# Scaling an expert's gathered token rows on ScalarE beside their transposes, in place of GpSimd behind the gather

## Chip, core and metric

The kernel is one program on one core of a Trainium2 chip. TensorE (PE, with its weight loads as PEld), VectorE (DVE), ScalarE (ACT), GpSimd (POOL) and the DMA queues of SyncE (SP) and GpSimd run side by side, each with its own list of instructions in a fixed order. The metric is the device time of one execution in microseconds (us).

## What is computed

A hybrid mixer block, then two layers of which the second ends in a mixture of experts; only that last part is touched by the change:

```
logits = t @ router_w;  top_logits, top_idx = top_k(logits, 2);  top_w = softmax(top_logits)
gates  = sum over k of top_w[:, k] * one_hot(top_idx[:, k])          # 512 tokens x 8 experts
for e in range(8):
    y = y + gates[:, e:e+1] * ((silu(t @ wg[e]) * (t @ wu[e])) @ wd[e])
```

`t` (512 x 1024) is an RMS norm of the residual rows times a column weight plus a column shift, and `wg`, `wu` are 1024 x 1408, `wd` is 1408 x 1024, all float32.

## The kernel before, in words

**Tokens are gathered by expert.** The normalised rows are written to a DRAM buffer `hnd` without their norm factor. For each expert a list of its token numbers (`ii`) and one norm factor for each token (`sc`) are made on chip. `fetch` (L1552) issues an indirect DMA on GpSimd's queue for each tile of tokens, which gathers the tokens' rows of 4 KB from `hnd` into `row`, 128 or 64 tokens by 1024. Then the rows are multiplied by `sc`: on GpSimd at L1563, or, for the first expert only (`now`), on ScalarE and VectorE. `inputs` (L1635) transposes `row` on TensorE, 16 blocks of 128 columns or fewer, and ScalarE and VectorE split the result into `eh` (high part) and `el` (low part).

**Two sizes of expert, taken in turns.** The experts are sorted by how many tokens they have. The first four have 192 places, as tiles of 128 and 64 (wide below); the last four have one tile of 128 (narrow). They are taken in the order `(0, 4, 1, 5, 2, 6, 3, 7)`, so a wide one and a narrow one take turns. During an expert the tokens of the one after it are prepared: `prepare(nxt)` and `fetch` stand in the program behind block `b == 0` (L1724), and `inputs` behind the first half of the last product (`m == 0`, L1742). A narrow expert so fetches two tiles, and a wide one fetches one.

**One expert.** Gate and up products run in three column blocks of 512, 512 and 384 (`b`). Each block takes eight weight chunks (`raw`, 128x1024, and 128x768 for the last block), and the down product takes twelve. `wload` (L235) does the same for each chunk: SP starts the load, ScalarE rounds it to `hi` (L205), VectorE makes `lo = raw - hi` (L216), TensorE multiplies by `hi` and by `lo`. There are 8 buffers for `raw` and 4 each for `hi` and `lo`. After a block ScalarE takes the silu of the gate (named `eh` too in the records, 128x512 from `g`), VectorE multiplies it by up (`eh<-g,eh`), and TensorE transposes the product (L1716 `m<-cst,eh`) for the down product (`th`, `tl`). The result is scaled and added into DRAM by an indirect DMA of GpSimd (`yd<-row`, L1755).

**What sets the order.** A scheduler puts each engine's instructions in a list when the program is built, with the chunk's load, `hi` and `lo` at high priority. On the chip an engine takes its list as it stands.

Of the kernel before, what the change touches and what calls it, by code (L numbers as in the profile page):

```python
# [13 lines left out]
AF = mybir.ActivationFunctionType  # L14
OP = mybir.AluOpType
# [4 lines left out]
D = 1024  # L20
# [154 lines left out]
def tile_kernel(ctx, tc, I, out, dbg=None, upto=99):  # L175
    nc = tc.nc
# [13 lines left out]
    def G(n=512):  # L190
        return pg.tile([128, n], F, tag="g", name="g")
# [5 lines left out]
    def act(o, i, f, bias=None, scale=None, accum=None):  # L197
        kw = {}
        if bias is not None:
            kw["bias"] = bias  # L200
        if scale is not None:
            kw["scale"] = scale
        if accum is not None:
            kw["accum_out"] = accum
        return nc.scalar.activation(out=o, in_=i, func=f, **kw).ins  # L205

    def stt(o, a, s, b, op0, op1):
        return nc.vector.scalar_tensor_tensor(out=o, in0=a, scalar=s, in1=b, op0=op0, op1=op1).ins  # L208

    def ts(o, a, s1, s2=None, op0=OP.mult, op1=None):  # L210
        if op1 is None:
            return nc.vector.tensor_scalar(out=o, in0=a, scalar1=s1, scalar2=None, op0=op0).ins
        return nc.vector.tensor_scalar(out=o, in0=a, scalar1=s1, scalar2=s2, op0=op0, op1=op1).ins
# [21 lines left out]
    def wload(src, n, after=()):  # L235

        fast["i"] += 1
        i = fast["i"]
        with ExitStack() as order:
            order.enter_context(tc.high_priority())  # L240
            for a in after:
                order.enter_context(tc.issue_after(a))
            p = fast["raw"] if fast["raw"] is not None and i % 2 else rawp
            raw = p.tile([128, 1024], F, tag="raw", name="raw")
            d = nc.sync.dma_start(out=raw[:, 0:n], in_=src)
            if i <= KD:
                tc.keep_in_program_order(d)
            hi = wsp.tile([128, 1024], R, tag="hi", name="hi")
            lo = wsp.tile([128, 1024], R, tag="lo", name="lo")
            act(hi[:, 0:n], raw[:, 0:n], AF.Copy)  # L250
            tt(lo[:, 0:n], raw[:, 0:n], hi[:, 0:n].bitcast(F), OP.subtract)
        return hi, lo
# [945 lines left out]
    with ExitStack() as st:  # L1198
# [321 lines left out]
        def dispatch(pays, n0, n, OH, a=0, b=8):  # L1520
            ps = M(8)[0:n]
            mm(ps[:, a:b], idb[:, 0:n], cw[:, n0 // 128, a:b], True, False)
            for t in range(NT):
                mm(ps[:, a:b], OH[:, t, n0:n0 + n], pays[:, t, a:b], False, t == NT - 1)
            return ps
# [3 lines left out]
        def slots(n, ps, real):  # L1529

            ii = lp.tile([n, 1], I32, tag=f"ii{n}", name="ii", bufs=3)
            with nc.allow_low_precision("small integers"):
                last[0] = nc.vector.reduce_sum(out=ii, in_=ps[:, 0:2], axis=AX.X).ins
            fi = None
            if real:
                fi = lp.tile([n, 1], F, tag=f"fi{n}", name="fi", bufs=2)
                nc.vector.reduce_sum(out=fi, in_=ps[:, 0:2], axis=AX.X)
            sc = lp.tile([n, 1], F, tag=f"sc{n}", name="sc", bufs=3)
            nc.vector.reduce_sum(out=sc, in_=ps[:, 2:5], axis=AX.X)
            return ii, fi, sc  # L1540
# [11 lines left out]
        def fetch(tiles, now=False):  # L1552

            for t_ in tiles:
                nc.gpsimd.indirect_dma_start(out=t_[4], out_offset=None, in_=hnd,
                                             in_offset=bass.IndirectOffsetOnAxis(ap=t_[2][:, 0:1], axis=0))
            for t_ in tiles:
                r, sc = t_[4], t_[5]
                if now:
                    act(r[:, 0:512], r[:, 0:512], AF.Copy, scale=sc[:, 0:1])  # L1560
                    ts(r[:, 512:1024], r[:, 512:1024], sc[:, 0:1])
                else:
                    nc.gpsimd.tensor_tensor(out=r, in0=r, in1=sc[:, 0:1].to_broadcast([t_[0], D]), op=OP.mult)  # L1563

        def places(P, W, off=0.0):
            OH = lp.tile([128, NT, 192], BF, tag="OH", name="OH", bufs=1)
# [4 lines left out]
        def prepare(r):  # L1571
            W = 192 if r < 4 else 128
            OH = places(P1r[:, r, :], W)
            return [tile_of(pay[:, r], n0, min(128, W - n0), OH, r == 7) for n0 in range(0, W, 128)]
# [5 lines left out]
        for n0, n in ((0, 128), (128, 64)):  # L1580
            ii, fi, sc = slots(n, dispatch(pay[:, 0], n0, n, OH0, 0, 5), False)
# [37 lines left out]
    with ExitStack() as st:  # L1619
# [3 lines left out]
        def hw(tag, shape=(128, T), dt=F):  # L1623
            return hp.tile(list(shape), dt, tag=tag, name=f"e{tag}")
# [10 lines left out]
        def inputs(tiles):  # L1635

            xs, pins = [], []
            for t_ in tiles:
                if t_[0] == 128:
                    e = wk.tile([128, 8, 128], R, tag="eh", name="eh", bufs=2)  # L1640
                    xs.append(([e[:, 0:4, :], e[:, 4:8, :]], two(("l2", "l3", "l4", "l5"))))
                else:
                    xs.append((two(("l6", "l7", "h6", "h7")), None))
            for m in range(2):
                for t_, (eh, el) in zip(tiles, xs):
                    n, xg = t_[0], t_[4]
                    ps = M(4 * n)
                    for k in range(4):
                        z = 512 * m + 128 * k
                        nc.tensor.transpose(ps[:, n * k:n * k + n], xg[:, z:z + 128], ident[0:n, 0:n])  # L1650
                    pv = ps.rearrange("p (k t) -> p k t", t=n)
                    hi, lo = (eh[m], el[m]) if n == 128 else (eh[m][:, :, 0:64], eh[m][:, :, 64:128])
                    b = [B[:, 4 * m + k:4 * m + k + 1] for k in range(4)]
                    for k in range(4):
                        pa = act(hi[:, k, :], pv[:, k, :], AF.Identity, bias=b[k])
                    for k in range(4):
                        pd = stt(lo[:, k, :], pv[:, k, :], b[k], hi[:, k, :].bitcast(F), OP.add, OP.subtract)
                pins.append((pa, pd))
            return xs, pins

        def emm(ps, a, b, hi, lo, first, last):
            mm(ps, a, hi, first, False)
            mm(ps, a, lo, False, last and b is None)
            if b is not None:
                mm(ps, b, hi, False, last)

        def whole(ps, n):

            lo = hw("h3")[0:64, 0:n]
            act(lo, ps[64:128, 0:n], AF.Copy)  # L1670
            turn["s"] = 1 - turn.get("s", 0)
            o = hw(("h4", "h5")[turn["s"]])[0:64, 0:n]
            tt(o, ps[0:64, 0:n], lo, OP.add)
            return o

        def expert(e, tiles, out_, nxt=None, beside=None):
# [10 lines left out]
            after = None  # L1687
            for b, w in enumerate((512, 512, 384)):
# [17 lines left out]
                for i, n in enumerate(ns):  # L1706
# [7 lines left out]
                    m = w // 128  # L1714
# [9 lines left out]
                if b == 0:  # L1724
                    if nxt is not None:
                        after = [prepare(nxt)]
                        fetch(after[0])
            yts = [row(n) for n in ns] if out_ is None else None
            for m in range(2):
                yp = [G() for n in ns]  # L1730
                for k0 in range(0, 11, 2):
                    kn = min(2, 11 - k0)
                    src = I["e_d"][bass.ds(e, 1), m, :, 512 * k0:512 * (k0 + kn)]
                    hi, lo = wload(src.rearrange("a p n -> (a p) n"), 512 * kn)
                    for r in range(kn):
                        k = k0 + r
                        z = slice(512 * r, 512 * r + 512)
                        for i in range(len(ns)):
                            th, tl = hs[i]
                            emm(yp[i], th[:, k, :], tl[:, k, :] if tl is not None else None, hi[:, z], lo[:, z],  # L1740
                                k == 0, k == 10)
                if m == 0 and after is not None:  # L1742
                    after.append(inputs(after[0]))
                for i, n in enumerate(ns):
                    p = yp[i] if n == 128 else whole(yp[i], 512)
                    iw = tiles[i][1][:, 0:1]
                    if out_ is None:
                        stt(yts[i][:, 512 * m:512 * m + 512], p, iw, g2[m][0:n], OP.mult, OP.mult)
                    else:
                        y = hw("h1")  # L1750
                        stt(y, p, iw, g2[m], OP.mult, OP.mult)
                        out_(m, y, tiles[i])
            if out_ is None:
                for i, n in enumerate(ns):
                    nc.gpsimd.indirect_dma_start(  # L1755
                        out=yd, out_offset=bass.IndirectOffsetOnAxis(ap=tiles[i][2][:, 0:1], axis=0),
# [134 lines left out]
```

## Time and profile before

| What | Value |
|---|---|
| Median of three runs | 1772.07 us (1770.12 to 1777.74) |
| The profiled execution | 1773.76 us, of which the span from first to last instruction is 1771.9 us |
| TensorE busy | 1717.7 us, 97% of the span |
| VectorE, ScalarE, GpSimd busy | 1234.7, 852.8, 78.6 us |
| Mean granted TensorE clock | 0.989 |

A busy time is the union of an engine's instructions; the end of a matmul is modelled, so a row's start says more than its end. The arrow in a row's brackets, as `[1.36 <-DVE lo L216]`, gives the engine's idle time ahead of that instruction and what ended it. `hi`, `lo`, `row` are names of tiles without their buffer numbers, and L205, L208, L212, L216, L219 are the lines of helpers, so that instructions are told apart by their tiles.

### The profile page before, as it was taken

What the parts mean: (1) busy time and instruction counts of PE and PEld (TensorE: products, weight loads), DVE (VectorE), ACT (ScalarE), POOL (GpSimd) and SP (SyncE); (2) the same over time, 40 slices, a digit from 0 to 9 for tenths busy, and PEclk for the clock granted to TensorE, in tenths of its full rate; (3) what the DMA queues carried; (4) which work ended last, traced back from release to release, by engine and by line L of the source; (5) the groups of instructions that cost most, each with busy time, mean ns of one, the idle gap of its engine ahead of it and who ended that gap; (6) DMA issues with size and microseconds to landing.
All of it is one profiled execution on the core that took longest, in us unless ns stands there. A gap on an engine that the chain in (4) does not pass through costs nothing. (4 is left out here: it accounts for less than half of the span.)

```text
span 1771.9 us, 24089 instructions
## 1 busy us (share of the span) xinstructions
PE 1717.7 (97%) x8580; PEld 1411.9 (80%) x8580; DVE 1234.7 (70%) x2065; ACT 852.8 (48%) x1326; POOL 78.6 (4%) x90
## 2 busy tenths in 40 slices
PE   8999998998999999999999999999999999999996
PEld 7867787786788888888888888787887887887884
DVE  6887789857567666443346766646788789788787
ACT  5435336745443222232333222535667567567575
POOL 1000001000000000000010000000011011011000
PEclk9999999999999999999999999999999999999998
DMA  8434641344426777333242111106789789789785
GB/s 270 137 112 136 226 126 59 118 153 158 132 88 221 250 240 244 115 98 91 97 142 73 48 60 60 48 24 244 258 279 339 228 281 334 228 283 338 228 282 226
DMA packets 95701, 313.47 MB, mean 177 GB/s; under 512 B 10772, under 2 KB 11284, under 8 KB 95576
## 3 DMA queue, kind: packets, MB, share of 16 engines
q1 hardware_dynamic: 89864, 295.88, 50.1%
q0 software_dynamic: 3408, 11.80, 3.1%
q10 hardware_dynamic: 2304, 4.20, 0.6%
q8 instruction: 69, 1.13, 0.3%
q14 instruction: 56, 0.46, 0.1%
HBM read 299.25 MB, written 12.58 MB: 176 GB/s over the span
## 5 line engine op out<-in xcount | busy, mean ns | idle before, releaser
L205 ACT ACTIVATE hi<-raw 128x1024 fp32r<-128x1024 f32 (+3 forms) x481 | 477.5, 996 | 592.8 <-PE g L219 474.4
L216 DVE TENSOR_TENSOR lo<-raw,hi 128x1024 fp32r<-128x1024 f32 (+3 forms) x481 | 551.5, 1158 | 288.0 <-ACT hi L205 278.0
L219 PE MATMUL g<-xh,hi 128*128 128x512 f32 (+1 forms) x912 | 354.8, 391 | 10.5 <-ACT hi L205 5.4
L219 PE MATMUL g<-xl,hi 128*128 128x512 f32 (+1 forms) x912 | 356.1, 391 | 1.0 <-DVE xl L208 0.8
L219 PE MATMUL g<-xh,lo 128*128 128x512 f32 (+1 forms) x912 | 356.4, 391 | 0.0
L219 PEld LDWEIGHTS g<-xh,hi 128*128 128x128 f32 x912 | 172.6, 190 | 45.2 <-ACT xh L205 6.0
L219 PEld LDWEIGHTS g<-xl,hi 128*128 128x128 f32 x912 | 173.0, 190 | 36.5 <-DVE xl L208 2.4
L219 PEld LDWEIGHTS g<-xh,lo 128*128 128x128 f32 x912 | 172.9, 190 | 33.4 <-issue 1.1
L219 PE MATMUL g<-lo,eh 128*128 128x512 f32 (+1 forms) x480 | 180.9, 377 | 4.7 <-DVE lo L216 4.7
L219 PE MATMUL g<-hi,eh 128*128 128x512 f32 (+1 forms) x480 | 180.1, 376 | 0.0
L219 PE MATMUL g<-hi,el 128*128 128x512 f32 (+1 forms) x480 | 167.1, 379 | 0.0
L378 DVE SCALAR_TENSOR_TENSOR ar<-ar,one,crow 128x1024 f32<-128x1024 f32 x96 | 122.1, 1283 | 29.0 <-DMA ar<-in_ada_dram 26.4
L219 PEld LDWEIGHTS g<-lo,eh 128*128 128x128 f32 x480 | 90.4, 188 | 19.6 <-DVE lo L216 5.6
L219 PE MATMUL g<-hi,th 128*128 128x512 f32 x264 | 105.0, 398 | 0.2
L219 PE MATMUL g<-lo,th 128*128 128x512 f32 x264 | 103.7, 393 | 0.0
L219 PEld LDWEIGHTS g<-hi,eh 128*128 128x128 f32 x480 | 90.5, 189 | 14.1
L219 PEld LDWEIGHTS g<-hi,el 128*128 128x128 f32 x480 | 90.0, 189 | 13.5
L219 PE MATMUL g<-fh,hi 128*128 128x512 f32 (+1 forms) x198 | 73.1, 369 | 0.0
L219 PE MATMUL g<-fl,hi 128*128 128x512 f32 (+1 forms) x198 | 72.7, 367 | 0.0
L219 PE MATMUL g<-fh,lo 128*128 128x512 f32 (+1 forms) x198 | 72.7, 367 | 0.0
L219 PE MATMUL g<-hi,tl 128*128 128x512 f32 x176 | 69.3, 395 | 0.0
L219 PE MATMUL g<-hi,xh 128*128 128x512 f32 (+1 forms) x160 | 60.2, 376 | 2.2 <-ACT x L205 1.4
(471 smaller groups left out, 2529.2 us busy)
## 6 DMA issues: line engine op xcount, KB each, us to landing
raw<-in_e_a_dram SPq DMA_DIRECT2D x128, 512.0 KB, 5.3
ar<-in_ada_dram SPq DMA_DIRECT2D x96, 512.0 KB, 4.4
raw<-in_e_d_dram SPq DMA_DIRECT2D x80, 512.0 KB, 5.5
raw<-in_e_b_dram SPq DMA_DIRECT2D x64, 384.0 KB, 6.2
raw<-in_f_gu_dram SPq DMA_DIRECT2D x44, 512.0 KB, 3.6
raw<-in_w_in_dram SPq DMA_DIRECT2D x22, 512.0 KB, 3.4
raw<-in_f_d_dram SPq DMA_DIRECT2D x16, 512.0 KB, 3.6
raw<-in_h_fq_dram SPq DMA_DIRECT2D x16, 512.0 KB, 3.3
```

Of the source, the lines that this page charges most:

```text
L205: return nc.scalar.activation(out=o, in_=i, func=f, **kw).ins
L216: return nc.vector.tensor_tensor(out=o, in0=a, in1=b, op=op).ins
L219: nc.tensor.matmul(o, l, r, start=start, stop=stop)
L378: nc.vector.scalar_tensor_tensor(out=raw, in0=raw, scalar=pace["one"], in1=crow, op0=OP.mult, op1=OP.mult, accum_out=mods[:, l, i, j:j + 1])
```

## The change

The multiply on GpSimd behind the gather is taken out. In its place ScalarE scales each tile of rows in place, with one activation over all 1024 columns, in the program just ahead of `inputs`, whose transposes read the rows.

```diff
                 if now:
                     act(r[:, 0:512], r[:, 0:512], AF.Copy, scale=sc[:, 0:1])
                     ts(r[:, 512:1024], r[:, 512:1024], sc[:, 0:1])
-                else:
-                    nc.gpsimd.tensor_tensor(out=r, in0=r, in1=sc[:, 0:1].to_broadcast([t_[0], D]), op=OP.mult)
...
-                if m == 0 and after is not None:
+                if m == 0 and after:
+                    for t_ in after[0]:
+                        act(t_[4], t_[4], AF.Copy, scale=t_[5][:, 0:1])
                     after.append(inputs(after[0]))
```

Where the scheduler puts the new activations is seen in the engines' lists. The first place is ScalarE's list in the first narrow expert, in its 384-column block; `hi<-raw 128x768` are this block's chunks, `eh...<-g` the silu of the block before, and `row<-row,sc` the new scaling.

```order
 L205 ACTIVATE hi<-raw 128x1024 x3
-L205 ACTIVATE eh_10967<-g 128x512
-L205 ACTIVATE hi<-raw 128x768 x5
+L205 ACTIVATE eh_10965<-g 128x512
+L205 ACTIVATE hi<-raw 128x768 x2
+L205 ACTIVATE row<-row,sc 128x1024
+L205 ACTIVATE hi<-raw 128x768 x2
+L205 ACTIVATE row<-row,sc 64x1024
+L205 ACTIVATE hi<-raw 128x768
 L205 ACTIVATE th<-m 128x512
 L205 ACTIVATE hi<-raw 128x768 x3
```

The scaling of 128 rows now stands ahead of the third chunk's `hi`, and that of 64 rows ahead of the fifth's, not behind the down product's first half. The second and the third narrow expert have the same rows.

The second place is VectorE's list at the same point; `OH` is a small mask for the next dispatch.

```order
 L212 TENSOR_SCALAR OH<-cst,P1r 128x128
 L216 TENSOR_TENSOR lo<-raw,hi 128x768
-L212 TENSOR_SCALAR OH<-cst,P1r 128x128 x2
-L216 TENSOR_TENSOR lo<-raw,hi 128x768
-L216 TENSOR_TENSOR eh_10967<-g,eh_10967 128x512
+L212 TENSOR_SCALAR OH<-cst,P1r 128x128 x3
+L216 TENSOR_TENSOR lo<-raw,hi 128x768
+L216 TENSOR_TENSOR eh_10965<-g,eh_10965 128x512
 L216 TENSOR_TENSOR lo<-raw,hi 128x768 x2
 L216 TENSOR_TENSOR tl<-m,th 128x512
```

One mask has moved up; the product `eh<-g,eh` stands right behind the third chunk's `lo`, as before.

The third place is ScalarE's list in the second wide expert, around the silu of its second block (`eh...<-g 128x512`).

```order
 L205 ACTIVATE hi<-raw 128x1024 x2
-L205 ACTIVATE eh_11609<-g 128x512
-L205 ACTIVATE hi<-raw 128x1024
-L205 ACTIVATE eh_11619<-g 64x512
-L205 ACTIVATE hi<-raw 128x768
-L205 ACTIVATE eh_11627<-eh_11621 64x512
+L205 ACTIVATE row<-row,sc 128x1024
+L205 ACTIVATE hi<-raw 128x1024
+L205 ACTIVATE eh_11608<-g 128x512
+L205 ACTIVATE eh_11618<-g 64x512
+L205 ACTIVATE hi<-raw 128x768
+L205 ACTIVATE eh_11626<-eh_11620 64x512
```

There the scaling has come in ahead of a chunk's `hi` and of the silu; the two wide experts after it have the same rows, and the first wide expert has it three rows further down. TensorE's list and SP's list hold the same instructions in the same order as before.

## Rows read from the trace of the kernel before

**Rows 1.** Windows: a narrow, a wide expert; PE, PEld, DVE, ACT, POOL, clock, DMA share.

```profile
1306.00:1366.00 60.00, 58.39 (x284) 48.04 (x283) 57.21 (x77) 45.50 (x64) 10.73 (x7) 1.00 0.98 348
1366.00:1438.00 72.00, 72.00 (x350) 60.47 (x349) 51.52 (x70) 42.81 (x60) 4.76 (x3) 1.00 0.74 227
```

**Rows 2.** Waits of TensorE, 1306 to 1704 us: total, times, longest.

```profile
PE g L219 <- DVE lo L216: 4.7, 3, 2.0
PE m L1716 <- DVE eh L216: 0.7, 3, 0.3
```

**Rows 3.** Timeline of TensorE at the first narrow expert's stop: start, length, instruction.

```profile
1334.72 0.34 PE L219 MATMUL g<-hi,el 128*128 128x384 f32 x1
1334.90 0.34 PE L219 MATMUL g<-hi,eh 128*128 128x384 f32 x1
1336.60 0.44 PE L219 MATMUL g<-lo,eh 128*128 128x384 f32 x1 [1.36 <-DVE lo L216]
```

**Rows 4.** Timeline of VectorE in the first narrow expert.

```profile
1326.53 0.27 DVE L212 TENSOR_SCALAR OH<-cst,P1r 128x128 bf16<-128x128 f32 x1
1326.72 0.95 DVE L216 TENSOR_TENSOR lo<-raw,hi 128x768 fp32r<-128x768 f32 x1
...
1328.85 0.68 DVE L216 TENSOR_TENSOR eh<-g,eh 128x512 f32<-128x512 f32 x1
...
1331.85 1.99 DVE L216 TENSOR_TENSOR lo<-raw,hi 128x768 fp32r<-128x768 f32 x1
1333.76 1.92 DVE L212 TENSOR_SCALAR OH<-cst,P1r 128x128 bf16<-128x128 f32 x1
```

**Rows 5.** Timeline of GpSimd: gathers and multiplies of narrow, wide, narrow, narrow.

```profile
1323.28 1.31 POOL L1555 DMA_INDIRECT row<-hnd,ii  x1 [4.63 <-PE g L219]
...
1330.79 2.23 POOL L1563 TENSOR_TENSOR row<-row,sc 128x1024 f32<-128x1024 f32 x1 [3.53 <-DMA row<-hnd,ii]
1333.70 1.89 POOL L1563 TENSOR_TENSOR row<-row,sc 64x1024 f32<-64x1024 f32 x1 [0.68 <-DMA row<-hnd,ii]
...
1386.74 1.89 POOL L1563 TENSOR_TENSOR row<-row,sc 128x1024 f32<-128x1024 f32 x1 [4.12 <-DMA row<-hnd,ii]
...
1464.45 4.30 POOL L1563 TENSOR_TENSOR row<-row,sc 128x1024 f32<-128x1024 f32 x2 [5.06 <-DMA row<-hnd,ii]
...
1596.35 1.93 POOL L1563 TENSOR_TENSOR row<-row,sc 128x1024 f32<-128x1024 f32 x1 [4.09 <-DMA row<-hnd,ii]
```

**Rows 6.** Timeline of ScalarE in the first narrow expert.

```profile
1324.64 1.74 ACT L205 ACTIVATE hi<-raw 128x768 fp32r<-128x768 f32 x2 [0.31 <-DMA raw<-in_e_b_dram]
```

**Rows 7.** ScalarE by form, 1306 to 1704 us: count, busy, mean ns, idle before.

```profile
L205 ACT ACTIVATE hi<-raw 128x1024 fp32r<-128x1024 f32 x157 | 165.8, 1060 | 78.9 <-PE g L219 66.5 <-DVE lo L216 4.8 <-ACT eh L205 3.5
L205 ACT ACTIVATE hi<-raw 128x512 fp32r<-128x512 f32 x12 | 7.6, 631 | 4.8 <-PE g L219 4.7
```

**Rows 8.** The tile row: the first expert's scaling on ScalarE, ns min/median/max.

```profile
L205 ACT ACTIVATE row<-row,sc x2: 722/732/742, 1217.0 to 1220.1; 128x512 f32<-128x512 f32 x1, 64x512 f32<-64x512 f32 x1
```

**Rows 9.** Timeline of TensorE: silu product's transposes in the three narrow experts.

```profile
1329.58 0.66 PE L1716 MATMUL m<-cst,eh 128*128 128x128 f32 x4
...
1461.97 0.60 PE L1716 MATMUL m<-cst,eh 128*128 128x128 f32 x4
...
1594.84 0.60 PE L1716 MATMUL m<-cst,eh 128*128 128x128 f32 x4
```

**Rows 10.** Timeline of ScalarE in the second wide expert.

```profile
1383.52 1.06 ACT L205 ACTIVATE hi<-raw 128x1024 fp32r<-128x1024 f32 x1 [1.23 <-PE g L219]
```

**Rows 11.** Timeline of TensorE, then windows at both clock levels, early in the program.

```profile
336.94 0.50 PE L219 MATMUL g<-lo,xh 128*128 128x512 f32 x1 [2.29 <-DVE lo L216]
...
338.30:341.60 3.30, 3.18 (x8) 2.51 (x9) 3.09 (x6) 1.04 (x3) 0.00 (x0) 0.50 0.47 166
341.70:345.00 3.30, 3.30 (x16) 2.73 (x15) 2.76 (x6) 1.39 (x2) 0.00 (x0) 1.00 0.00 0
1469.60:1476.00 6.40, 6.37 (x30) 5.60 (x31) 6.40 (x6) 4.11 (x6) 0.00 (x0) 1.00 0.99 370
```

## Prediction

> **What bounds the kernel now.** I read the mixture of experts alone, since the change touches nothing ahead of it, and began with busy times in windows of one expert [rows 1]. The reader is to see two regimes. A wide expert has TensorE busy in all of its 72 us, while ScalarE has 29 us and VectorE 20 us to spare. A narrow one has TensorE at 58.4 of 60 us, VectorE at 57.2 and the DMA engines at 0.98: everything is nearly full, and little is needed to make TensorE stop. What stops TensorE is in its waits [rows 2]: from 1306 to 1704 us it stood for VectorE's `lo` three times, 4.7 us in all, and for `eh` three times, 0.7 us, once in each narrow expert. Nothing else held it. So the time of this stretch is TensorE's work plus these stops, and whatever adds a stop adds time.
>
> Why `lo` is late is seen on VectorE [rows 4] beside GpSimd [rows 5]. A `lo` of 768 columns takes 0.95 us at 1326.72 but 1.99 us at 1331.85, while GpSimd multiplies from 1330.79 to 1333.02. A mask takes 0.27 us at 1326.53 but 1.92 us at 1333.76, beside GpSimd's 1.89 us from 1333.70. So each multiply holds VectorE up for most of its own length, and the last two of them make the 1.36 us stop of TensorE at 1336.60 [rows 3].
>
> **The change part by part.**
>
> *Removed: ten multiplies on GpSimd.* Four stand in wide experts, where the hold-up ends in VectorE's spare time: worth nothing there. The six in narrow experts cause the stops. Matmuls of 384 columns start 0.18 us apart, and the stop lies between starts at 1334.90 and 1336.60 [rows 3], so it costs 1.70 - 0.18 = 1.52 us, 0.16 more than the idle time in its row. For three experts that is 4.7 + 3 x 0.16 = 5.2 us. The 0.7 us behind `eh` follow from VectorE's backlog and may go or stay; I count 0.4. Gain: 5.6 us (bounds 0 and 5.9).
>
> *Added: ten activations on ScalarE.* No row shows 128x1024 with a scale column. The plain rounding takes 1.06 us; at 512 columns a scale column makes 0.73 of 0.63 us [rows 7, 8], so I take 1.06 + 0.10 = 1.15 us (bounds 1.06, as without the column, and 1.46, two of the 512 kind). The 11.5 us of work themselves are hidden: ScalarE spent 66.5 us waiting for TensorE ahead of 1024-column roundings alone [rows 7].
>
> *Moved: the wait for the gather.* It was at the head of GpSimd's list, with nothing urgent behind it: 3.53, 5.06 and 4.09 us idle in the narrow experts [rows 5]. Now it is in ScalarE's list, where the lists show the third chunk's `hi` behind it, and behind that on VectorE the third `lo` and the silu product `eh`, and behind that on TensorE the transposes L1716, and with them all later matmuls. In the first narrow expert ScalarE is through with the second `hi` at 1324.64 + 1.74 = 1326.38 [rows 6], while the rows land only when GpSimd's multiply could start, at 1330.79. So ScalarE stands 4.4 us. What follows is a chain: scaling 1.15, `hi` of 768 columns 0.87 (two took 1.74 [rows 6]), `lo` 0.95, `eh` 0.68 [rows 4], and 0.1 for handing over, 3.75 us in all (bounds 3.66 and 4.06). The transposes then start at 1330.79 + 3.75 = 1334.54 and not at 1329.58 [rows 9]: TensorE stops for 5.0 us. In the second narrow expert the landing is 1464.45 and the transposes were at 1461.97: 1468.20 - 1461.97 = 6.2 us. In the third 1596.35 and 1594.84: 1600.10 - 1594.84 = 5.3 us [rows 5, 9]. Sum: 16.5 us.
>
> Could the landings move? The gathers are issued at the places they had, ahead of the first difference in that expert's lists, and share the DMA engines with loads already on their way. I keep them.
>
> The second scaling (64 rows, landed by 1333.70 [rows 5]) stops nothing more: behind the stop ScalarE has done the third and the fourth `hi` at 1333.7, the scaling by 1334.85 and the fifth `hi` by 1335.7, its `lo` by 1336.7. TensorE at 1334.54 has four transposes (0.4 us), then four matmuls of the second chunk and six each of the third and the fourth, 16 x 0.18 = 2.9 us, and needs the fifth at 1337.8.
>
> SP's loads wait for `lo` to free one of eight buffers, so from the third `lo` on they leave up to 5 us later. That lies under the stop: what those buffers hold or have on its way is not used up when the stop ends, and TensorE asks for the later chunks some 3 us later than it did.
>
> In the wide experts the scaling comes ahead of a `hi` and a silu. ScalarE would get there at 1383.52 + 1.06 = 1384.6 and stand until 1386.74 [rows 5, 10], so the next `hi` ends at about 1389.0. There are four `hi` buffers, ScalarE waits for TensorE to free one, and a chunk lasts 2.0 us on the mean (72 us [rows 1] over 16 + 8 + 12 chunks), so a `hi` is ready about three chunks, 6 us, before its use. The new one comes 2 to 3 us later. Hidden. If that cover were gone, three experts at 2 to 3 us each would be 6 to 9 us more.
>
> *The clock.* A stop of 5 to 6 us is longer than any in rows 2. What a shorter one did is seen early in the program [rows 11]: TensorE stood 2.29 us ahead of 336.94, and soon after the granted clock was 0.50, the level of 1.2 GHz, with 8 matmuls in 3.3 us, against 16 in the next 3.3 us at 1.00, the level of 2.4 GHz. So such a stretch costs about 1.7 us of work. After the 1.96 us stop that ended at 1469.63 the clock stayed at 1.00. I take one stretch for each stop: 3 x 1.7 = 5.1 us (bounds 0, and 10.2 for two each). The Trainium skill, "TensorE: Matmul & The Clock Gate", section "What's actually happening", says that the slow clock is the default and that activity releases it, a rule that speaks against this change. By the rule each long stop is paid twice, by trace rows after shorter stops sometimes; the two sums differ by just these 5.1 us.
>
> *Sum.* 16.5 - 5.6 + 5.1 = +16.0 us. The profiled execution took 1773.76 us, so 1789.8 for it; the median of the runs is 1.7 us lower, so the forecast is 1772.1 + 16.0 = 1788.1 us.
>
> **The rivals.**
>
> *A: only the relief stays (faster).* If the gathered rows land before ScalarE asks for them, TensorE loses nothing and VectorE is no longer held up: 1772.1 - 5.6 = 1766.5 us. It turns where the three stops together come to 5.6 us, so with landings (16.5 - 5.6) / 3 = 3.6 us earlier, 1327.2 in place of 1330.79, 2.6 us after GpSimd finished issuing at 1324.59 [rows 5]. For it speaks the clear hold-up of VectorE; against it that all six landings kept GpSimd waiting, with DMA engines 0.98 busy. 5 in 100. The Trainium skill, "GPSIMD Engine Reference", section "Specifications", has GpSimd share its memory interfaces with VectorE, to the cost of instructions with two inputs in SBUF, as `lo` is; the trace agrees (0.95 against 1.99 us), and by that rule alone this case would come.
>
> *B: the stop is paid back (no change).* If a narrow expert is in truth set by the DMA engines at 0.98 [rows 1], TensorE's stop uses time in which chunks would have been late anyway: half of 16.5 us comes back, the clock holds: 1772.1 + 8.2 - 5.6 = 1774.7 us. Against it: in rows 2 no wait of TensorE ends in a load, and the wide expert behind has TensorE full, so nothing can be caught up there. 10 in 100.
>
> *C: the stops as forecast, the clock stays up.* 1772.1 + 10.9 = 1783.0 us. For it speaks the stop of 1.96 us without a slow stretch [rows 11]; against it that the new stops are over twice as long. 20 in 100.
>
> *D: more than that.* Two slow stretches for each stop, or chunks that come late behind it since their loads left late: 1772.1 + 10.9 + 10.2 = 1793 us, with a few more for late loads up to 1800. 8 in 100.
>
> **How the numbers follow.** The forecast has 57 in 100, with 1784 to 1793 of its own (the chain's bounds give -0.4 and +1.1, the gain's +5.6 and -0.3, the clock some 2 us either way). A change can be told from none at about 0.5%, 9 us, so at 1781 and above. C and D lie above it, C closely: of its 20 I put 16 there. Slower: 57 + 16 + 8 = 81, rounded to 80; within: B, the rest of C and some: 15; faster: 5. The range of 1780 to 1797 holds the forecast's case, most of C and of D, and leaves out A and B.
>
> **What would show it.** In the profile after: no multiply on GpSimd, no `lo` of 768 columns near 2 us; ScalarE idle ahead of `row<-row,sc` by 4 to 7 us, ended by the gather's DMA, three times in narrow experts and about 2 us in wide ones; TensorE idle ahead of L1714 (the transposes' new line) by 5 to 6 us, ended by `eh` of VectorE, three times; the three waits for `lo` gone; granted clock 0.50 behind those stops; wide experts still full. The forecast is wrong if the gathers land sooner, if TensorE has other work ahead of the transposes, or if the narrow experts end no later in spite of the stop.

## The result and the profile after

| | before | after |
|---|---|---|
| Median of nine runs each | 1772.07 us (1767.65 to 1778.7) | 1786.33 us (1781.15 to 1793.1) |
| Profiled execution | 1773.76 us | 1784.45 us, span 1782.7 us |
| GpSimd, VectorE, ScalarE busy | 78.6, 1234.7, 852.8 us | 56.8, 1223.5, 862.0 us |

The ratio is 1.0081, with a 95% interval of 1.0064 to 1.0098: slower, by 14.3 us between the medians. 1788.1 us was forecast.

The program ahead of the experts is untouched, yet in the nine profiled executions of this study the first expert's scatter begins anywhere from 1302 to 1310 us. A whole time carries that spread. So I measure the **stretch** from the start of the first expert's scatter (`yd<-row`, L1755) to that of the fourth wide one's, which holds three narrow experts and three wide ones. There is one trace of each kernel. How far a stretch can be trusted is seen in its three wide experts, where the kernels hardly differ: from scatter to scatter they take 217.7 to 218.0 us together in seven traces and 218.5 in one (in the ninth, of the late kernel below, the narrow experts' scatters lie elsewhere). In windows (length, then busy time of PE, PEld, DVE, ACT, POOL, the granted clock, DMA share, GB/s) it reads, for the kernel before:

```profile
1305.78:1703.32 397.54, 392.09 (x1898) 326.83 (x1897) 327.88 (x434) 266.01 (x367) 47.92 (x27) 1.00 0.85 282
```

And for the kernel after, the stretch first, then the windows that answer to [rows 1], then pieces behind TensorE's stops:

```profile
1302.08:1713.72 411.64, 398.02 (x1898) 334.04 (x1897) 316.69 (x434) 274.27 (x376) 29.81 (x19) 0.98 0.84 272
...
1306.00:1366.00 60.00, 55.61 (x267) 46.59 (x266) 51.04 (x73) 43.91 (x61) 3.92 (x4) 0.97 0.95 332
1366.00:1438.00 72.00, 72.00 (x350) 60.50 (x349) 50.33 (x69) 43.71 (x61) 3.06 (x2) 1.00 0.73 228
...
1330.63:1333.85 3.22, 3.22 (x12) 3.22 (x13) 2.01 (x3) 3.10 (x4) 0.00 (x0) 0.50 0.80 232
1333.90:1340.00 6.10, 6.10 (x36) 5.98 (x35) 5.63 (x7) 5.60 (x7) 0.00 (x0) 1.00 0.88 285
1467.70:1473.80 6.10, 6.10 (x21) 6.10 (x22) 4.31 (x5) 3.61 (x6) 0.00 (x0) 0.50 0.85 269
...
1605.14:1610.30 5.16, 5.16 (x18) 5.16 (x19) 3.90 (x5) 3.25 (x5) 0.00 (x0) 0.50 0.88 262
```

The stretch has grown by 411.64 - 397.54 = 14.1 us. The first two numbers of a row split it: TensorE idle went from 397.54 - 392.09 = 5.45 to 13.62 us (+8.2), TensorE busy from 392.09 to 398.02 us (+5.9) with the same 1898 matmuls. So the loss has two parts, standing and slower work. The wide expert is still full, 72.00 of 72. The narrow one has lost 2.8 us of TensorE's busy time in 60. GpSimd is nearly empty and VectorE has 6 us less to do, and it did not help.

Who TensorE waits for, in the waits from 1306 to 1715 us of the kernel after, where [rows 2] had two lines:

```profile
PE m L1714 <- DVE eh L216: 13.6, 3, 5.1
```

The `lo` line is gone. The waits for `eh` are 13.6 us in place of 0.7, but they are not the old ones grown longer. In the kernel before, they lay ahead of the third block's transposes (three, x3); the second block's (four, x4, [rows 9]) came without a wait. TensorE's timeline of the kernel before, the matmul ahead of 1329.58 and the wait:

```profile
1329.30 0.34 PE L219 MATMUL g<-lo,eh 128*128 128x384 f32 x1
...
1344.30 0.52 PE L1716 MATMUL m<-cst,eh 128*128 128x128 f32 x3 [0.23 <-DVE eh L216]
```

Now TensorE waits ahead of the second block's transposes. TensorE's timeline of the kernel after (start, length, instruction, in brackets the idle time and its end):

```profile
1325.92 0.34 PE L219 MATMUL g<-hi,eh 128*128 128x384 f32 x1
1330.63 1.12 PE L1714 MATMUL m<-cst,eh 128*128 128x128 f32 x4 [4.37 <-DVE eh L216]
...
1467.70 1.12 PE L1714 MATMUL m<-cst,eh 128*128 128x128 f32 x4 [5.06 <-DVE eh L216]
...
1605.14 1.12 PE L1714 MATMUL m<-cst,eh 128*128 128x128 f32 x4 [4.13 <-DVE eh L216]
```

From start to start, less the usual 0.18 us, the first stop is 4.53 us, 0.16 more than its idle time. With 0.16 for each of the others too, the three come to 13.6 + 0.5 = 14.0 us. What is behind them stands in ScalarE's timeline (three rows of the first narrow expert, one of a wide one, one each of the other narrow ones):

```profile
1327.10 1.15 ACT L205 ACTIVATE row<-row,sc 128x1024 f32<-128x1024 f32 x1 [4.46 <-DMA row<-hnd,ii]
1328.15 1.56 ACT L205 ACTIVATE hi<-raw 128x768 fp32r<-128x768 f32 x2
1330.73 1.15 ACT L205 ACTIVATE row<-row,sc 64x1024 f32<-64x1024 f32 x1 [1.01 <-DMA row<-hnd,ii]
...
1386.83 1.15 ACT L205 ACTIVATE row<-row,sc 128x1024 f32<-128x1024 f32 x1 [2.10 <-DMA row<-hnd,ii]
...
1464.17 1.15 ACT L205 ACTIVATE row<-row,sc 128x1024 f32<-128x1024 f32 x1 [5.15 <-DMA row<-hnd,ii]
...
1601.61 1.15 ACT L205 ACTIVATE row<-row,sc 128x1024 f32<-128x1024 f32 x1 [4.22 <-DMA row<-hnd,ii]
```

And in VectorE's, behind ScalarE's `hi`:

```profile
1329.01 0.96 DVE L216 TENSOR_TENSOR lo<-raw,hi 128x768 fp32r<-128x768 f32 x1 [4.79 <-ACT hi L205]
1329.89 0.68 DVE L216 TENSOR_TENSOR eh<-g,eh 128x512 f32<-128x512 f32 x1
```

The reader is to see one delay handed on: the gather's DMA ends ScalarE's wait at 1327.10, `hi` follows at 1328.15, `lo` at 1329.01, `eh` at 1329.89, the transposes at 1330.63. All three engines show an idle time of 4.4 to 4.8 us, but only the first ends in a transfer. TensorE's own row names VectorE, which was itself waiting.

VectorE's groups by form show that the relief came: the mean of a `lo` of 768 columns is 957 ns, so none near the 1.99 us of [rows 4].

```profile
L216 DVE TENSOR_TENSOR lo<-raw,hi 128x768 fp32r<-128x768 f32 x48 | 45.9, 957 | 32.7 <-ACT hi L205 31.8 <-PE g L219 0.5
```

### The profile page after: what moved, and what is told of

Its sections match the earlier page's. It is cut to its first block, busy times and chain, and to the rows that moved or that the text cites. A ratio compares the mean times of both kernels' runs of the same rounds, so it can differ in the third digit from the quotient of the medians.

```text
span 1782.7 us, 24084 instructions
## 1 busy us (share of the span) xinstructions
PE 1721.2 (97%) x8580; PEld 1417.8 (80%) x8580; DVE 1223.5 (69%) x2065; ACT 862.0 (48%) x1336; POOL 56.8 (3%) x80
## 5 line engine op out<-in xcount | busy, mean ns | idle before, releaser
L216 DVE TENSOR_TENSOR lo<-raw,hi 128x1024 fp32r<-128x1024 f32 (+3 forms) x481 | 544.5, 1142 | 317.1 <-ACT hi L205 306.7
L219 PEld LDWEIGHTS g<-hi,el 128*128 128x128 f32 x480 | 92.0, 193 | 13.6
L219 PE MATMUL g<-lo,xh 128*128 128x512 f32 (+1 forms) x160 | 59.0, 369 | 2.3 <-DVE lo L216 2.3
```

Of the source, the lines that this page charges most:

```text
L216: return nc.vector.tensor_tensor(out=o, in0=a, in1=b, op=op).ins
L219: nc.tensor.matmul(o, l, r, start=start, stop=stop)
```

## The experiments

Each kernel starts from the changed one, and its ratio is to the kernel before. The stretch is told as length, idle and busy time of TensorE.

**The change without any scaling behind the gather.** No row of an expert but the first's is multiplied by its norm factor: this part of the computation is left out. This gives what taking the multiplies off GpSimd is worth by itself.

```diff
                 if m == 0 and after:
-                    for t_ in after[0]:
-                        act(t_[4], t_[4], AF.Copy, scale=t_[5][:, 0:1])
                     after.append(inputs(after[0]))
```

> No scaling by the norm factor at all for the experts after the first (this part of the computation is left out). It gives the worth of the multiplies on GpSimd alone. If they hold VectorE up and so stop TensorE: 1766.5 us and 391.7 us between the same scatters, without a wait of TensorE for VectorE in the narrow experts. If they cost nothing: 1772 us and 397.5 us.

Measured: 1769.51 us, ratio 0.9993 (0.9979 to 1.0007). The stretch in windows:

```profile
1306.65:1700.18 393.53, 391.22 (x1898) 327.22 (x1897) 317.27 (x434) 266.19 (x367) 29.68 (x18) 1.00 0.86 285
```

The same kernel, waits of TensorE:

```profile
PE m L1714 <- DVE eh L216: 2.3, 3, 0.8
```

4.0 us shorter than before. The `lo` stops are gone, but the waits for `eh`, 0.7 us before, are now 2.3: they lie at the third block's product, some 7 us behind the place of the `lo` stops. Part of the gain is given back there, so the gain is 4.0 us and not 5.6. The whole time doesn't show it: its interval holds 1, and 1766.5 us was expected. The 4.0 us rest on the stretch, of one trace each.

**The work alone, and the wait alone.** Both leave the rows unscaled and put something at the two places of ScalarE's list where the change has its scalings in a narrow expert. The first has an activation of the same size on a tile that nothing else touches: all the work, no wait. The second copies one column of the gathered tile: the wait, nearly no work.

```diff
+                        if b == 2 and g == 0 and q in (1, 3) and len(ns) == 1 and after:
+                            t_ = after[0][q // 2]
+                            with tc.issue_after(fast["hi"]):
+                                act(idle[0:t_[0], :], idle[0:t_[0], :], AF.Copy, scale=1.0)
```

```diff
+                                act(peek[0:t_[0], q // 2:q // 2 + 1], t_[4][:, 0:1], AF.Copy)
```

> The scalings of the narrow experts stay at their place in ScalarE's list and keep their size, but work on a tile that waits for nothing (the rows themselves are not scaled, and in wide experts nothing is done). If the wait is the cost: as without any scaling, 1766.5 us and 391.7 us between the scatters. If ScalarE's work is the cost: near 1786 us, 411 us.

> At the same place in ScalarE's list one column of the gathered tile is read instead, so the wait is there without the work (the rows are not scaled). If the wait is the cost: the three stops stay and are 1 us shorter each, 3.4, 4.1 and 3.3 us, with the slow clock behind them in part: 1766.5 + 10.8 + 5 = 1782 us, 407 us between the scatters. If the work is the cost: 1766.5 us, 391.7 us.

Measured for the work: 1770.05 us, ratio 0.9989 (0.9974 to 1.0003); its stretch in windows:

```profile
1304.23:1700.57 396.34, 392.31 (x1898) 326.98 (x1897) 316.98 (x434) 270.60 (x373) 30.53 (x19) 1.00 0.85 283
```

The same kernel, waits of TensorE:

```profile
PE m L1720 <- DVE eh L216: 3.1, 3, 1.1
PE g L219 <- DVE lo L216: 0.9, 2, 0.6
```

The same kernel, timeline of ScalarE:

```profile
1324.69 1.05 ACT L205 ACTIVATE idle<-idle 128x1024 f32<-128x1024 f32 x1
```

Measured for the wait: 1788.38 us, ratio 1.0094 (1.0069 to 1.0119); its stretch in windows:

```profile
1307.64:1717.77 410.13, 398.54 (x1898) 331.44 (x1897) 317.18 (x434) 266.36 (x373) 29.39 (x18) 0.99 0.84 273
```

The same kernel, waits of TensorE:

```profile
PE m L1719 <- DVE eh L216: 11.5, 3, 4.4
```

The same kernel, timeline of ScalarE:

```profile
1332.87 0.20 ACT L205 ACTIVATE peek<-row 128x1 f32<-128x1 f32 x1 [4.38 <-DMA row<-hnd,ii]
1332.98 1.56 ACT L205 ACTIVATE hi<-raw 128x768 fp32r<-128x768 f32 x2
```

A copy of 0.20 us costs nearly what the change costs: 410.13 us against 393.53 without it, so 16.6 us (407 us was expected of the copy); 0.8 of them lie in the wide experts, where this kernel has no copy. The activations without a wait cost 396.34 - 393.53 = 2.8 us. They took 1.05 us each, since they have no scale column, and not the 1.15 us of the change. It is the wait, not the work, though the work is not quite free there.

**Each kind of fetch by itself.** ScalarE scales only the rows of fetches of two tiles, which lie in narrow experts, or only those of one tile, which lie in wide ones; GpSimd multiplies the others as before. The diff is that for two tiles alone; the other kernel has `== 2` in its first line and `== 1` in the second `if`.

```diff
+                elif len(tiles) == 1:
+                    nc.gpsimd.tensor_tensor(out=r, in0=r, in1=sc[:, 0:1].to_broadcast([t_[0], D]), op=OP.mult)
...
+                    if len(after[0]) == 2:
+                        for t_ in after[0]:
+                            act(t_[4], t_[4], AF.Copy, scale=t_[5][:, 0:1])
```

> The change for the fetches of two tiles alone, which lie in the narrow experts; the fetches of one tile (in the wide experts) are scaled on GpSimd as before. If all of the time is lost where ScalarE comes to the scaling of the narrow experts: as the change, about 1786 us, with three stops of TensorE of 4 to 5.5 us and 411 to 412 us from the first expert's scatter to the fourth wide one's. If the wide experts' part of the change costs or brings something: off that by as much, and the next run off the kernel before by the same with the other sign.

> The change for the fetches of one tile alone, which lie in the wide experts; the fetches of two tiles are scaled on GpSimd as before. If the change in the wide experts is hidden: as the kernel before, 1770 to 1773 us, about 397.5 us from the first expert's scatter to the fourth wide one's, and no stop above those of before. If a wait of ScalarE for a transfer costs there too: stops of TensorE in the wide experts, and 2 us or more each.

Measured for two tiles: 1784.91 us, ratio 1.0069 (1.0047 to 1.0092). The three stops are there, 12.5 us in its waits, and end at 1338.05, 1474.27 and 1610.36; windows of the stretch, and behind the stops:

```profile
1309.69:1718.10 408.41, 395.84 (x1898) 332.04 (x1897) 319.39 (x434) 270.81 (x373) 36.81 (x22) 0.99 0.83 274
...
1338.38:1341.78 3.40, 3.40 (x13) 3.40 (x12) 2.17 (x4) 3.18 (x5) 0.00 (x0) 0.50 0.82 259
1341.80:1345.00 3.20, 3.20 (x19) 3.20 (x19) 2.58 (x4) 2.78 (x5) 0.00 (x0) 1.00 0.86 252
1474.91:1478.31 3.40, 3.40 (x13) 3.40 (x12) 2.44 (x4) 3.16 (x5) 0.00 (x0) 0.50 0.81 259
1611.45:1614.85 3.40, 3.40 (x13) 3.40 (x12) 3.06 (x4) 1.82 (x3) 0.00 (x0) 0.50 0.83 286
```

Measured for one tile: 1772.88 us, ratio 0.9998 (0.9982 to 1.0014); the stretch in windows:

```profile
1305.56:1702.52 396.96, 392.13 (x1898) 327.08 (x1897) 323.54 (x434) 268.57 (x370) 44.01 (x25) 1.00 0.83 282
```

The same kernel, waits of TensorE:

```profile
PE g L219 <- DVE lo L216: 4.1, 3, 1.4
PE m L1716 <- DVE eh L216: 0.7, 3, 0.2
```

The same kernel, timeline of ScalarE:

```profile
1386.31 1.15 ACT L205 ACTIVATE row<-row,sc 128x1024 f32<-128x1024 f32 x1 [2.13 <-DMA row<-hnd,ii]
```

In the wide experts ScalarE stands 2.13 us for the gather and TensorE doesn't notice: from scatter to scatter the three take 218.0 us, 217.8 before. All the loss lies in the narrow ones. The stretch with two tiles alone is 408.41 us, not the 411 to 412 expected, and the 3.2 us between it and the change are not the wide experts', which take 217.7 us here and 217.9 in the change. Its stops are 1.1 us shorter in sum, and the slow clock is shorter. The granted clock fell 0.3, 0.6 and 1.1 us after TensorE had resumed, and was back 3.4 us later each time. In the change it fell while TensorE still stood, 0.2, 0.7 and 1.6 us before it resumed, and was back after 3.4, 6.8 and 6.8 us. Windows of the change, the two long ones, which begin inside the stops that end at 1467.70 and 1605.14:

```profile
1467.00:1473.82 6.82, 6.12 (x21) 6.12 (x22) 5.01 (x7) 4.33 (x6) 0.00 (x0) 0.50 0.80 256
1603.54:1610.35 6.81, 5.21 (x18) 5.21 (x19) 5.55 (x7) 4.85 (x6) 0.00 (x0) 0.50 0.85 272
```

So the long ones are the two in which the clock fell well inside the stop. What sets the moment of its fall, no run here shows.

**The stops filled.** 18 matmuls of 128x512 that nothing reads stand in TensorE's list where it stopped, ahead of the transposes; ScalarE and VectorE keep their lists. In the diff, `held[0]()` is those transposes and `FILL` is 18.

```diff
+                            if b == 2 and g == 0 and k == 3 and held:
+                                fp, x0 = M(512), xs[0][0][0]
+                                for f in range(FILL):
+                                    with tc.issue_after(pm_[0]):
+                                        pm_[0] = mm(fp, x0[:, 0, :], x0.rearrange("p k t -> p (k t)"), f == 0, f == FILL - 1)
+                                with tc.issue_after(pm_[0]):
+                                    held[0]()
```

> The change, with 18 more matmuls of 128x512 (18 x 0.228 = 4.1 us) in TensorE's list ahead of the transposes that stop there, so that the stop is filled with work that nothing reads; the output is the reference's. If the slower clock behind each stop adds to it, as the prediction has it: the granted clock stays at 1.00 behind the filled stops and some 7 us come back, about 1779 us and 404 to 405 us from the first expert's scatter to the fourth wide one's. If the clock plays no part: as the change, about 1786 us and 411 to 412 us.

Measured: 1783.1 us, ratio 1.0064 (1.0037 to 1.009), which overlaps the interval of the change, so the stretch decides. Windows of the stretch and behind the three places:

```profile
1305.11:1712.28 407.17, 403.65 (x1952) 337.50 (x1951) 316.03 (x434) 273.34 (x376) 29.92 (x18) 1.00 0.82 275
...
1334.00:1340.00 6.00, 6.00 (x37) 6.00 (x38) 5.27 (x7) 6.00 (x9) 0.00 (x0) 1.00 0.84 270
1471.00:1478.00 7.00, 6.92 (x41) 6.92 (x42) 6.53 (x9) 6.59 (x10) 0.00 (x0) 1.00 0.88 292
1606.00:1612.00 6.00, 6.00 (x37) 6.00 (x37) 5.53 (x7) 5.59 (x8) 0.00 (x0) 1.00 0.85 272
```

The same kernel, timeline of TensorE:

```profile
1329.00 4.25 PE L219 MATMUL m<-eh 128*128 128x512 f32 x18
1333.87 0.66 PE L1724 MATMUL m<-cst,eh 128*128 128x128 f32 x4 [0.62 <-DVE eh L216]
...
1471.08 0.66 PE L1724 MATMUL m<-cst,eh 128*128 128x128 f32 x4 [2.63 <-DVE eh L216]
```

The same kernel, timeline of ScalarE in the second narrow expert:

```profile
1467.55 1.15 ACT L205 ACTIVATE row<-row,sc 128x1024 f32<-128x1024 f32 x1 [6.63 <-DMA row<-hnd,ii]
```

54 matmuls more (x1952 against x1898), and the stretch is 4.5 us shorter than the change's 411.64. The clock stays at 1.00 behind all three places. Without the filling (54 x 0.228 us from start to start = 12.3 us) TensorE is busy 403.65 - 12.3 = 391.3 us against 398.0 in the change: 6.7 us of slow clock are gone. Filling and idle time together are 12.3 + 3.5 = 15.8 us against 13.6 idle in the change, which is why 4.5 us came back and not 6.7. The filling did not run over the stops: behind it TensorE still waited for `eh` at each place, 0.62, 2.63 and 0.21 us. In the second narrow expert the gather landed later, so that ScalarE stood 6.63 us there against 5.15 in the change, and the transposes came 30.73 us behind the scatter against 29.28. The rest is one matmul of 0.18 us at each place, which stands ahead of the transposes in the change and behind them here.

**The scaling later.** The change, with the scalings queued on ScalarE behind the third block's silu.

```diff
-                    act(s, gp, AF.Silu)
+                    sil = act(s, gp, AF.Silu)
...
-                    for t_ in after[0]:
-                        act(t_[4], t_[4], AF.Copy, scale=t_[5][:, 0:1])
+                    with tc.issue_after(sil):
+                        for t_ in after[0]:
+                            act(t_[4], t_[4], AF.Copy, scale=t_[5][:, 0:1])
```

> The change, but each scaling on ScalarE is queued behind the silu of the expert's third block, when the gathered rows have long landed. If the wait for the gather is the cost: TensorE has no stop behind the silu product in the narrow experts and none behind a held-up VectorE, so 1772 - 5.6 = 1766.5 us, faster than both kernels; from the first expert's scatter to the fourth wide expert's (397.5 us before, 411.6 after) 391.7 us. If ScalarE's ten extra activations are the cost (11.5 us of work): still 1783 us or more, about 409 us. If the multiplies on GpSimd cost nothing: 1772 us, 397.5 us.

Measured: 1765.28 us, ratio 0.996 (0.9943 to 0.9978) against the kernel before: 5.5 us under the median of 1770.75 us that it had beside it, and so faster than both kernels. The stretch in windows:

```profile
1309.09:1702.72 393.63, 392.19 (x1898) 327.02 (x1897) 316.39 (x434) 273.09 (x376) 27.43 (x18) 1.00 0.86 285
```

The same kernel, waits of TensorE:

```profile
PE g L219 <- DVE lo L216: 1.3, 3, 0.8
```

The same kernel, timeline of ScalarE:

```profile
1338.85 1.06 ACT L205 ACTIVATE hi<-raw 128x1024 fp32r<-128x1024 f32 x1
1339.82 1.14 ACT L205 ACTIVATE row<-row,sc 128x1024 f32<-128x1024 f32 x1
1340.86 1.04 ACT L205 ACTIVATE hi<-raw 128x1024 fp32r<-128x1024 f32 x1
```

ScalarE comes to the scaling at 1339.82 with nothing in brackets: the rows have landed. From the first expert's scatter that is 1339.82 - 1309.09 = 30.7 us. In the change ScalarE came there at 20.6 us (1327.10 - 4.46 - 1302.08), and the rows landed at 25.0. The stretch is 393.63 us, that of the kernel without any scaling to 0.1 us. So the move to ScalarE is worth all of its 4 us; what lost 18 us was the place in the list. One thing doesn't fit: the median is 4.2 us under that of the kernel without any scaling, though the stretches agree. The execution traced took 1773.53 us, 8 us above the median, so its trace can't show where the time was gained.

## Why the prediction was right

The mechanism was the forecast's: the stretch grew by 14.1 us where the sum said 16.0, and the median by 14.3. That the sum came so near is in part luck: the wait was 2.5 us too large and the clock 1.5 us too small. By its steps:

- **The moved wait**, 16.5 us forecast, is 14.0. ScalarE does come to the rows before they land, at each of the three places, and `hi`, `lo`, `eh` and the transposes follow as listed. The wait by itself makes 16.6 us of stretch, clock included. The term was oversized in two places. The chain from landing to transposes took 3.53 us each time (1327.10 to 1330.63), not 3.75, since successive rows of an engine overlap by 0.1 us and I added whole lengths: 0.7 us in all. And the landings came 1.00, 1.69 and 0.76 us behind the moment when TensorE ran dry (start of the transposes less the stop), while [rows 5, 9] give 1.21, 2.48 and 1.51: 1.75 us. Together 2.4 of the 2.5 us. About half of the 1.75 us comes from TensorE's order, which is not quite that of before, as it was put ahead of the prediction: in the traces the transposes stand behind ten matmuls of the 384-column block in all three narrow experts, behind eight before, and so 0.35 us of work stands ahead of each stop that stood behind the transposes before.
- **The clock**, 5.1 us forecast, is 6.6. The pieces at 0.50 behind the three stops hold 3.22 + 6.10 + 5.16 = 14.5 us, and not quite half of that is lost, since matmuls of 384 columns start 0.32 us apart there against 0.18 at 1.00. From the start of the transposes to the first matmul of 512 columns behind them it is 8.63, 9.94 and 9.54 us in the change; in the filled kernel it is 7.35 each time, 0.18 of it for one matmul more. The difference is 6.6 us in all; by the busy time against the filled kernel it was 6.7. One stretch of 3.3 us for each stop, taken from [rows 11], held for one of three. The Trainium skill, "TensorE: Matmul & The Clock Gate", section "What's actually happening", has the slow clock as the default that activity lifts; the trace agrees here, with 0.50 behind every long stop and 1.00 behind every filled one.
- **The gain on VectorE**, 5.6 us forecast, is 4.0 where nothing takes its place. The hold-up did end, as forecast, but the waits for `eh`, of which I counted 0.4 us as gone, grew from 0.7 to 2.3 us instead. In the change itself no such wait is left behind the longer stops.
- **The added work**, forecast as hidden, took 1.15 us each, as estimated. Nearly the same work (1.05 us each) costs 2.8 us at that place without any wait; 10 us later the scaling costs 0.1. ScalarE's idle time on the mean was no evidence for that one place, where `hi` stands ahead of `lo` and `eh`.
- **The wide experts and the second scaling** are hidden, as forecast: 2.10 us of waiting and no stop of TensorE there, and no fourth wait in its list. In the first narrow expert the 64 rows landed 3.6 us behind the 128 (2.9 in [rows 5]), so that ScalarE stood 1.01 us more, and it stopped nothing. Rival D's late chunks did not come.
- **Adding the terms:** 14.0 + 6.6 - 6.4 is 14.2 us against 14.1 measured. The 6.4 us are all idle time behind `lo` and `eh` of before, 5.4 us, with 0.16 us for each of six starts.

In the first narrow expert the landing kept its place, as the prediction took it. GpSimd's timeline of the kernel after:

```profile
1319.57 1.29 POOL L1555 DMA_INDIRECT row<-hnd,ii  x1 [4.56 <-PE g L219]
```

From this issue to the landing are 1327.10 - 1319.57 = 7.5 us, and 1330.79 - 1323.28 = 7.5 us in [rows 5]; there TensorE ran dry 0.2 us later. In the other two the landing came 0.4 us sooner after the expert's scatter and TensorE ran dry 0.4 us later.

Rival A needed landings before ScalarE asks; it waited 4.2 to 5.2 us. B is out, since nothing was paid back: the stops and the clock add up to the growth, and the wide experts take 217.9 us where they took 217.8. C is out by the filled kernel: the clock is part of the loss. D had the longer slow stretches right, but with stops shorter than forecast the time stayed under its 1793 us.

What stays open: what sets the moment at which the clock falls, and with it whether 3.4 or 6.8 us are slow. And in the kernel with the wait alone TensorE's busy time is 7.3 us above that of the kernel without it. The slow clock makes some 4.9 of them (9.1 us from the transposes to the first matmul of 512 columns, three times, against 7.5), and 0.8 lie in its wide experts at a clock of 1.00; the rest I can't place.

## What to carry to other kernels

A wait has a price by what is queued behind it. The same wait for a gather cost nothing at the head of GpSimd's idle list, nothing on ScalarE in a wide expert with a few chunks in hand, and about 16 us on ScalarE in the three narrow ones. So when an operation moves to another engine, first find when its input lands (issue to landing of the transfer), then put it in the new list behind that moment, not where its result could first be used: here 10 us later turned +14 us of the stretch into -4. And a stop of TensorE is priced with the slow clock that the profile shows behind it: here nearly 7 us on 14.

## What the runs showed of the hardware

- Three stops of 4.3 to 5.2 us were each followed by granted clock 0.50, for 3.2, 6.1 and 5.2 us of work; the same places filled with useless matmuls stayed at 1.00, and 54 matmuls more made the stretch 4.5 us shorter.
- The slow clock lasted twice as long where it fell well inside a stop (0.7 and 1.6 us before TensorE resumed: 6.8 us) as where it fell from 0.2 us before to 1.1 us after TensorE resumed (3.4 us, seven times in the change, the two-tiles kernel and the kernel with the wait alone).
